# Attention's gated sum put off, experts' weights split by whole chunks, one-hots begun earlier

## The chip, the cores and the metric

One NeuronCore of a Trainium2 chip runs the whole program. The metric is the device time of one execution in microseconds; of the profiled execution the span is told too, from the first to the last instruction. TensorE is PE, VectorE DVE, ScalarE ACT, GpSimd POOL; SP is the queue that issues most of the DMAs.

## What is computed

One layer over 1024 latent tokens of width 1024 with 256 context tokens: a normalized, modulated input goes through one projection into latent attention (8 heads, 128 + 64 wide keys) and a bidirectional mLSTM; both are gated, summed and projected, and a residual is added. Then a mixture of 16 SwiGLU experts follows in which each expert takes its best 128 tokens, and a last norm.

```python
y_mla = attend(q, concat([k_ctx, k_lat]), concat([v_ctx, v_lat]))        # softmax over 1280 keys
out   = (sigmoid(g_mla) * y_mla + sigmoid(g_ml) * y_ml) @ w_out
x     = x + g1 * out
aff   = softmax(h @ w_router);  g, idx = top_k(aff.T, 128)               # each expert picks its tokens
a, u  = xs @ w_e_gate, xs @ w_e_up                                       # xs = h[idx], 128 x 1024
y     = (silu(a) * u) @ w_e_down * g                                     # added back at idx
```

All matrix products of weights are done in three passes of a 32-bit format (fp32r): a value is split into a high part (ACT's cast) and a low part (DVE's subtraction of the cast from the value), and high x high, high x low and low x high are summed in PSUM.

## The kernel before

Each engine has one queue in order. The order in it is laid down when the program is built, by a planner that takes ready instructions by priority (program order, raised inside `high_priority`) against costs of its own; `issue_after(x)` makes what follows stand behind x on x's engine.

**Attention** (line 1425 on) goes in 32 steps g: head g // 4, 256 queries each. A step's `scores` makes five PSUM tiles of 128 keys x 2 and a running maximum over them on DVE: one reduction (1529), four `tensor_max` (1532), a halving (1536). `peak` turns the maximum on PE (1545) and reduces it (1548); `peak2` writes the row into the queries' extra rows (1560, 1561); `exps` adds it through PE, exponentiates on ACT, casts the high parts, and lets POOL sum the five exponentials (1590, 1592). Meanwhile the step before is finished: `low` makes low parts of its exponentials on DVE (1599), `values` and `values2` are PE's products, `weigh` and `weigh2` make the weight of a query out of the sum (1623 to 1630), and `finish` multiplies (1635) and adds the gated result to the accumulator in SBUF (1636).

**Experts.** `Weights` (line 770 on) streams 16 x 12 chunks of 1 MB (128 partitions x 2 x 1024): eight of gate and up (two halves of the hidden width, four chunks each), four of down. Raw chunks go round `N_RAW` = 16 buffers and two single ones (`ONCE`); `split` casts and subtracts half a chunk at a time (128 x 1024, lines 875 and 876) into a ring of `N_HI` = 4 pairs of high and low. `products` (1305) asks for the split of the half four ahead, for loads further on, and issues 12 matmuls of 512 columns a chunk (through the helper line 1190). `pick(e)` builds eight one-hot tiles 128 x 128 of the tokens of expert e on POOL (1257; on DVE for e = 0), multiplies them on PE with a table to get row numbers and gates (1263), makes these into integers on DVE (1270 to 1275) and gathers the rows by an indirect DMA of POOL (1278). `turn_x` and `turn` are PE transposes with a cast and a subtraction (1287 to 1290). `y` (1353) scales an expert's result, and POOL's indirect DMA adds it to DRAM (1354).

In the loop over experts the order is: four gate/up chunks, `act` (silu on ACT 1315, product on DVE 1316), four more with the transposes of the first hidden half inside, and `pick(e + 2)` after the second of these (the sixth chunk); then four down chunks D0 to D3 with the transposes of the second half after D0, and those of the next expert's tokens after D1 and D2; then `y` and the scatter.

Before the experts, `Merge.rest` prepares three half chunks with the subtraction on POOL (`W.split(N_HI - 1, G)`) while DVE sorts the routing weights; a fourth is split by DVE behind `counted`, and the slots of the tokens follow behind that.

Of the kernel before, what the change touches and what calls it, by code (L numbers as in the profile page):

```python
# [33 lines left out]
P = 128  # L34
# [24 lines left out]

N_HAP, N_EARLY, N_MID, N_LATE, N_HI = 2, 3, 4, 7, 4  # L60
N_RAW = N_HAP + N_EARLY + N_MID + N_LATE
# [708 lines left out]
class Weights:  # L770
# [34 lines left out]
    def load(self, upto):  # L805
        while self.loaded < min(upto, 12 * NE):
            j = self.loaded
            j = SEQ[j] if j < len(SEQ) else j
            src = self.source(j)
            if j in ONCE:  # L810
                t = self.once[j]
                loads = [self.nc.sync.dma_start(t[c], src[:, c, :]) for c in range(self.begun.pop(j, 0), 2)]
            else:
                b = self.buffer(SEQ.index(j) if j < len(SEQ) else j - 2)
                t = b[:, 0], b[:, 1]
                if len(b.shape) == 4:
                    src = src.rearrange("p a (c d) -> p a c d", d=256)
                loads = [self.nc.sync.dma_start(b, src)]
            if self.after is not None:
                for x in loads:  # L820
                    self.tc.add_manual_dep(x.ins, self.after.ins.name,
                                           mybir.DependencyInfo(mybir.DependencyClass.Sync, mybir.DependencyReason.DATA),
                                           reason="what is awaited goes before")
                if j >= N_RAW + 2 or j in (ONCE[0], 14, 15, 16, 17):
                    self.after = None
            self.raw[j] = t
            self.loaded += 1
# [30 lines left out]
    def halves(self):  # L858
        return [self.hi.tile([P, D], F32R, name=x, bufs=N_HI) for x in ("hi", "lo")]

    def split(self, upto, engine=None):

        while self.cut < min(upto, 24 * NE):
            j, c = divmod(self.cut, 2)
            self.load((SEQ.index(j) if j < len(SEQ) else j) + 1)
            w = self.raw[j][c]
            if self.cut < 24 * NE - 8:
                hi, lo = self.halves()
            else:
                both = self.buffer(self.cut - 12 * NE + 6, F32R)  # L870
                hi, lo = both[:, 0, :], both[:, 1, :]
            self.parts[self.cut] = hi, lo
            if len(w.shape) == 3:
                hi, lo = [t.rearrange("p (c d) -> p c d", d=256) for t in (hi, lo)]
            self.nc.scalar.copy(hi, w)  # L875
            done = (engine or self.nc.vector).tensor_sub(lo, w, hi)  # L876
            self.cut += 1
            if self.cut == upto:
                return done
# [90 lines left out]
class Merge:  # L970
# [81 lines left out]
    def rest(self, aff, thr, pool):  # L1052
# [109 lines left out]
        for i in range(8):  # L1162
            project(i)
            if i > 0:
                store_h(i - 1)
            if i < 7:
                self.source(i + 1)
            W.load((1, 3, 6, 6, 7, 7, 9, 9)[i])
        W.load(N_RAW - 1)
        self.sb.close()  # L1170
        W.hi = pool("p7a")
        t = W.wide_hi(F32)
        W.once[ONCE[0]] = t[:, 0, :], t[:, 1, :]
        W.split(N_HI - 1, G)
        with tc.high_priority():
# [9 lines left out]
def moe(tc, A, out, aff, thr, W, h2_d, acc_d, ident, rstd, dump):  # L1185
# [6 lines left out]
    with ExitStack() as st:  # L1192
# [43 lines left out]
        with tc.issue_after(counted.ins):  # L1236
            done = W.split(N_HI)

# [11 lines left out]
        V.scalar_tensor_tensor(slot, taken[:, :, 0, :], -1.0, taken[:, :, 1, :], op0=ALU.add, op1=ALU.add)  # L1250
        gat, idx, xg, xsT, hid = {}, {}, {}, {}, {}

        def pick(e):
            oh = W.narrow().bitcast(BF16).rearrange("p (a b) -> p a b", b=P)
            for o in range(8):
                if e > 0:
                    G.tensor_scalar(oh[:, o, :], iota, slot[:, o, e:e + 1], None, op0=ALU.is_equal)  # L1257
            for o in range(0, 8, 4) if e == 0 else ():
                V.tensor_tensor(oh[:, o:o + 4], iota[:, None, :].to_broadcast([P, 4, P]),
                                slot[:, o:o + 4, e:e + 1].to_broadcast([P, 4, P]), op=ALU.is_equal)  # L1260
            ap = ps7.tile([P, 512], F32, name="tr", bufs=2)
            for i in range(8):
                done = mm(ap[:, :5], oh[:, i, :], aux[:, i, e, :], i == 0, i == 7)
            if e == 0:
                with tc.issue_after(done.ins):
                    ps = ps7.tile([P, 512], F32, name="pu", bufs=2)
                    for x in range(11):
                        mm(ps, W.parts[0][0][:, :P], W.parts[0][0][:, :512], True, True)
            ax = p7.tile([P, 8], F32, name="ax", bufs=3)
            V.tensor_copy(ax[:, :5], ap[:, :5])  # L1270
            idx[e] = p7.tile([P, 1], I32, name="idx", bufs=4)
            gat[e] = p7.tile([P, 1], F32, name="gt", bufs=4)
            V.scalar_tensor_tensor(idx[e], ax[:, 0:1], 128.0, ax[:, 1:2], op0=ALU.mult, op1=ALU.add)
            V.tensor_add(gat[e], ax[:, 2:3], ax[:, 3:4])
            picked = V.tensor_add(gat[e], gat[e], ax[:, 4:5])
            dump("idx", idx[e], lambda o: o[:, e:e + 1])
            xg[e] = p7.tile([P, D], F32, name="xg", bufs=2)
            got = G.indirect_dma_start(out=xg[e], out_offset=None, in_=h2_d,
                                 in_offset=bass.IndirectOffsetOnAxis(ap=idx[e][:, :1], axis=0))
            with tc.issue_after(got.ins):  # L1280
                return picked, got, G.memset(ax[:, 7:8], 0.0)
# [15 lines left out]
        def products(j, ps, l, start, stop):  # L1297

            for c in range(2):
                W.split(2 * j + c + N_HI)  # L1300
                if c == 0:
                    W.load(N_RAW + j + 4 - sum(o < j + 2 for o in ONCE))
                wh, wl = W.parts.pop(2 * j + c)
                k = 2 * (j % 4) + c
                lh, ll = l[0][:, k, :], l[1][:, k, :]
                for o in range(2):
                    r = slice(o * 512, o * 512 + 512)
                    mm(ps[o], lh, wh[:, r], start and c == 0, False)
                    mm(ps[o], lh, wl[:, r], False, False)
                for o in range(2):  # L1310
                    mm(ps[o], ll, wh[:, slice(o * 512, o * 512 + 512)], False, stop and c == 1)

        def act(pa, pu):
# [3 lines left out]
            return h  # L1317

        picked, got, W.after = pick(0)
        for q in range(2):  # L1320
            turn_x(0, q)
        urgent.__exit__(None, None, None)
        with tc.issue_after(W.after.ins):
            pick(1)
        for e in range(NE):
# [3 lines left out]
            for hf in range(2):  # L1329
                ps = [ps7.tile([P, 512], F32, name=x, bufs=2) for x in ("pa", "pu")]  # L1330
                for q in range(4):
                    products(j + 4 * hf + q, ps, xsT[e], q == 0, q == 3)
                    if hf == 1 and q == (2 if e == 0 else 0):
                        t = W.wide_hi(F32R)
                        hd += [t[:, x, :].rearrange("p (a b) -> p a b", b=P) for x in range(2)]
                        turn(hs[0], *hd, 0)
                    if hf == 1 and q == 1 and e + 2 < NE:
                        pick(e + 2)
                hs.append(act(*ps))
            py = [ps7.tile([P, 512], F32, name=f"py{o}", bufs=1) for o in range(2)]  # L1340
            if e + 1 < NE:
                for q in range(4):
# [3 lines left out]
                    if q == 0:  # L1346
                        turn(hs[1], *hd, 1)
                    if q in (1, 2):
                        turn_x(e + 1, q - 1)
# [16 lines left out]
            for m in range(4):  # L1366
                x = W.middle(m)
                for a in range(2):
                    i = 2 * m + a
                    nc.sync.dma_start(x[:, a], acc_d[i * P:(i + 1) * P].rearrange("p (c d) -> p c d", d=256))  # L1370
                xs += [x[:, 0], x[:, 1]]
# [12 lines left out]
            def write(i):  # L1384
                scale(i, xs[i])
                stores.append(nc.sync.dma_start(out[i * P:(i + 1) * P].rearrange("p (c d) -> p c d", d=256), xs[i]))

            W.split(24 * NE)
            z = p7.tile([P, D], F32, name="xg", bufs=2)
            for o in range(2):  # L1390
                c = slice(o * 512, o * 512 + 512)
                for k in range(8):
                    wh, wl = [w[:, c] for w in W.parts[2 * j + 16 + k]]
                    mm(py[o], hd[0][:, k, :], wh, k == 0, False)
# [30 lines left out]
def attention(tc, A, xc, qn_d, qp_d, kv, kpe, g1_d, ident, ones, ml, weights, follow):  # L1425
# [12 lines left out]
    with tc.tile_pool(name="p5", bufs=1, reuse_waits="tile") as p5, \  # L1438
# [5 lines left out]
        NG = 4 * HEADS  # L1444
        vh, vl, K, Q, G1, PS, MX, TH, SUM, W, PV = {}, {}, {}, {}, {}, {}, {}, {}, {}, {}, {}

# [111 lines left out]
        def peak2(g):  # L1558
# [3 lines left out]
            with tc.issue_after(cut.ins):  # L1562
                for p in PARTS[2:]:
                    low(g - 1, p)

        def exps(g):
# [60 lines left out]
        def weigh2(g):  # L1627
            tr = along(*W[g])
            w = W[g] = p5.tile([P, 256], F32, name="w", bufs=2)
            V.tensor_mul(w, tr, G1[g // 2][:, cols(g)])  # L1630

        def finish(g):
            h, c = g // 4, slice((g % 4) * 256, (g % 4) * 256 + 256)
            w = W.pop(g)
            V.tensor_mul(w, PV.pop(g), w)
            V.tensor_add(xc[h][:, c], xc[h][:, c], w)

# [406 lines left out]
```

## Time and profile before

| | us |
|---|---|
| median of 3 runs (2039.46 to 2044.31) | 2041.03 |
| the profiled execution | 2041.3 |
| its span | 2039.5 |
| PE busy, share of the span | 1910.6, 94% |
| DVE busy | 1462.2, 72% |
| ACT busy | 1048.9, 51% |
| POOL busy | 602.0, 30% |
| mean granted clock of PE | 0.979 |

Shares are averages over stages with different limits; what a change in one stage is worth is read from that stage's own rows. In a timeline a row is: start, length, engine, line, operation, output and inputs, shapes, how many instructions were merged into the row, and in brackets how long the engine stood idle before it and what ended that.

### The profile page before, as it was taken

The numbers are of one execution on the slowest core, as the hardware profiler recorded it, in microseconds if no ns is written. First come the engines' busy times: TensorE is split into PE (matmuls) and PEld (weight loads), VectorE is DVE, ScalarE is ACT, GpSimd is POOL, SyncE is SP. The second block draws the span as 40 slices with busy tenths as digits, with TensorE's granted clock in tenths as the row PEclk, the third lists the DMA queues.
The fourth block names the chain that finished last, engine by engine and source line by source line (L and its number), as shares of the span: only waits on it lengthen the run. The fifth ranks groups of instructions, "written<-read, shape, count | busy, mean of one in ns | idle before, by whom it ended". The sixth has DMA issues, their size and how long they took to land. (4 is left out here: it accounts for less than half of the span.)

```text
span 2039.5 us, 28755 instructions
## 1 busy us (share of the span) xinstructions
PE 1910.6 (94%) x10458; PEld 1614.1 (79%) x10458; DVE 1462.2 (72%) x2704; ACT 1048.9 (51%) x1677; POOL 602.0 (30%) x527
## 2 busy tenths in 40 slices
PE   7999999999999999899999998985999999999994
PEld 3898888888877878889998987863778778787873
DVE  6454555112477888687877788578899999999997
ACT  5554421123247676434334434321777777777774
POOL 0000000000043040275434446433453634536310
PEclk9999999999999999999999998997999999999997
DMA  7143376222187060323111111636899999999975
GB/s 302 58 149 100 106 248 220 76 93 89 61 279 248 22 221 1 94 71 117 50 47 50 37 53 58 246 133 224 292 375 380 372 381 369 383 382 364 388 240 187
DMA packets 156301, 385.84 MB, mean 189 GB/s; under 512 B 10224, under 2 KB 94784, under 8 KB 137088
## 3 DMA queue, kind: packets, MB, share of 16 engines
q1 hardware_dynamic: 141104, 329.73, 44.9%
q0 software_dynamic: 12752, 45.90, 7.4%
q10 hardware_dynamic: 2304, 8.39, 1.1%
q8 instruction: 82, 1.34, 0.3%
q14 instruction: 59, 0.48, 0.1%
HBM read 327.04 MB, written 56.93 MB: 188 GB/s over the span
## 5 line engine op out<-in xcount | busy, mean ns | idle before, releaser
L86 PE MATMUL mm<-hT,whi 128*128 128x512 f32 (+1 forms) x1392 | 414.8, 381 | 2.6 <-DVE hT L305 2.3
L86 PEld LDWEIGHTS mm<-hT,whi 128*128 128x128 f32 x1392 | 255.1, 189 | 52.0 <-DVE hT L305 2.4
L86 PE MATMUL mm<-hT,wlo 128*128 128x512 f32 (+1 forms) x696 | 262.9, 378 | 0.3 <-DVE wlo L90 0.3
L876 DVE TENSOR_TENSOR lo<-raw_l,hi 128x1024 fp32r<-128x1024 f32 x156 | 188.1, 1235 | 11.2 <-ACT hi L875 8.2
L1257 POOL TENSOR_SCALAR g<-iota,slot 128x128 bf16<-128x128 f32 x120 | 192.4, 1624 | 0.0
L875 ACT CAST hi<-raw_l 128x1024 fp32r<-128x1024 f32 x156 | 163.3, 1053 | 48.2 <-PE pu L1190 33.8
L1190 PE MATMUL py<-hi,hd 128*128 128x512 f32 x480 | 160.8, 399 | 0.0
L86 PEld LDWEIGHTS mm<-hT,wlo 128*128 128x128 f32 x696 | 131.2, 189 | 24.5 <-DVE wlo L90 0.7
L90 DVE TENSOR_TENSOR wlo<-wraw,whi 128x1024 fp32r<-128x1024 f32 x38 | 46.5, 1224 | 142.8 <-ACT whi L89 142.8
L1590 POOL TENSOR_TENSOR es<-es,e 128x512 f32<-128x512 f32 x96 | 126.4, 1317 | 7.0
L1590 POOL TENSOR_TENSOR es<-e 128x512 f32<-128x512 f32 x32 | 41.8, 1305 | 272.4 <-ACT e L1584 272.4
L876 DVE TENSOR_TENSOR lo<-xca,hi 128x1024 fp32r<-128x1024 f32 x96 | 115.3, 1231 | 6.6 <-ACT hi L875 4.8
L1584 ACT ACTIVATE e<-s 128x512 f32<-128x512 f32 x160 | 94.5, 612 | 47.1 <-PE s L1432 47.1
L1354 POOL DMA_INDIRECT acc_d<-y,idx x15 | 34.9, 2328 | 270.4 <-DVE y L1353 270.4
L875 ACT CAST hi<-xca 128x1024 fp32r<-128x1024 f32 x96 | 100.1, 1051 | 27.6 <-PE pu L1190 20.0
L89 ACT CAST whi<-wraw 128x1024 fp32r<-128x1024 f32 x38 | 40.0, 1051 | 128.8 <-PE mm L86 120.4
L1190 PEld LDWEIGHTS py<-hi,hd 128*128 128x128 f32 x480 | 89.7, 188 | 17.9
L1190 PE MATMUL pa<-hi,xh 128*128 128x512 f32 x256 | 102.4, 400 | 0.3 <-ACT xh L1289 0.3
L1190 PE MATMUL pa<-lo,xh 128*128 128x512 f32 x256 | 99.9, 390 | 1.1 <-DVE lo L876 1.1
L1190 PE MATMUL pu<-lo,xh 128*128 128x512 f32 x256 | 99.8, 390 | 0.0
L1190 PE MATMUL pu<-hi,xl 128*128 128x512 f32 x256 | 99.8, 390 | 0.0
L1190 PE MATMUL pa<-hi,xl 128*128 128x512 f32 x256 | 99.7, 390 | 0.0
(509 smaller groups left out, 5088.2 us busy)
## 6 DMA issues: line engine op xcount, KB each, us to landing
raw_l<-in_wgu SPq DMA_DIRECT2D x54, 1024.0 KB
xca<-in_wgu SPq DMA_DIRECT2D x33, 1024.0 KB
raw_l<-in_wd SPq DMA_DIRECT2D x28, 1024.0 KB
raw_e<-in_wgu SPq DMA_DIRECT2D x24, 1024.0 KB
wraw<-in_win SPq DMA_DIRECT2D x38, 512.0 KB
wt<-in_wmod_b SPq DMA_DIRECT2D x32, 512.0 KB
ha<-in_wgu SPq DMA_DIRECT2D x16, 1024.0 KB
xca<-in_wd SPq DMA_DIRECT2D x15, 1024.0 KB
```

The costliest lines, as they stand in the source:

```text
L86: return TE.matmul(o, l, r, start=start, stop=stop, skip_group_check=True)
L89: S.copy(hi, raw)
L90: V.tensor_sub(lo, raw, hi)
L875: self.nc.scalar.copy(hi, w)
L876: done = (engine or self.nc.vector).tensor_sub(lo, w, hi)
L1190: return TE.matmul(o, l, r, start=start, stop=stop, skip_group_check=True)
L1257: G.tensor_scalar(oh[:, o, :], iota, slot[:, o, e:e + 1], None, op0=ALU.is_equal)
L1354: G.indirect_dma_start(out=acc_d, out_offset=bass.IndirectOffsetOnAxis(ap=idx[e][:, :1], axis=0), in_=y, in_offset=None, compute_op=ALU.add)
L1584: S.activation(E[p], ps, AF.Exp)
L1590: G.tensor_add(s, E[0] if p == 1 else s, E[p])
```

## The change

Three parts.

1. The addition of `finish` (line 1636) is no longer made at the end of its pass through the loop but in the `peak2` of the next pass, behind the low part that is made there; the last two steps add at once. The ring of the product has three buffers instead of two.
2. `split` casts and subtracts a whole chunk (128 x 2048) at a time; the ring holds three whole chunks (`N_HI` = 3) instead of four halves. The memory comes from the raw buffers: `N_EARLY` goes from 3 to 1, so `N_RAW` from 16 to 14. Before the experts, one whole chunk is prepared on POOL and a second on DVE, instead of three halves and one. The last expert's last chunks and the rows for the last norm move to other buffers.
3. `pick` is cut in two. `mark(e + 2)` builds the one-hots and is called after the fourth chunk of an expert; `pick(e + 2)`, the products with the table and the gather, is called after D1, the tenth.

```diff
-N_HAP, N_EARLY, N_MID, N_LATE, N_HI = 2, 3, 4, 7, 4
+N_HAP, N_EARLY, N_MID, N_LATE, N_HI = 2, 1, 4, 7, 3
...
     def halves(self):
-        return [self.hi.tile([P, D], F32R, name=x, bufs=N_HI) for x in ("hi", "lo")]
+        return [self.hi.tile([P, 2, D], F32R, name=x, bufs=N_HI) for x in ("hi", "lo")]
...
     def split(self, upto, engine=None):
-        while self.cut < min(upto, 24 * NE):
-            j, c = divmod(self.cut, 2)
+        while self.cut < min(upto, 12 * NE):
+            j = self.cut
             self.load((SEQ.index(j) if j < len(SEQ) else j) + 1)
-            w = self.raw[j][c]
-            if self.cut < 24 * NE - 8:
+            raw = self.raw[j]
+            if not 12 * NE - 4 <= j < 12 * NE - 2:
                 hi, lo = self.halves()
             else:
-                both = self.buffer(self.cut - 12 * NE + 6, F32R)
-                hi, lo = both[:, 0, :], both[:, 1, :]
-            self.parts[self.cut] = hi, lo
...
-            self.nc.scalar.copy(hi, w)
-            done = (engine or self.nc.vector).tensor_sub(lo, w, hi)
+                hi, lo = [self.buffer(2 * j - 12 * NE + 6 + x, F32R) for x in range(2)]
+            self.parts[j] = hi, lo
...
+            for h, l, w in views:
+                self.nc.scalar.copy(h, w)
+                done = (engine or self.nc.vector).tensor_sub(l, w, h)
...
-            W.load((1, 3, 6, 6, 7, 7, 9, 9)[i])
+            W.load((1, 3, 4, 4, 5, 5, 7, 7)[i])
...
-        W.split(N_HI - 1, G)
+        W.split(1, G)
...
         with tc.issue_after(counted.ins):
-            done = W.split(N_HI)
+            done = W.split(2)
...
-        def pick(e):
-            oh = W.narrow().bitcast(BF16).rearrange("p (a b) -> p a b", b=P)
+        def mark(e):
+            oh = marks[e] = W.narrow().bitcast(BF16).rearrange("p (a b) -> p a b", b=P)
             for o in range(8):
                 if e > 0:
                     G.tensor_scalar(oh[:, o, :], iota, slot[:, o, e:e + 1], None, op0=ALU.is_equal)
...
+        def pick(e):
+            oh = marks.pop(e)
             ap = ps7.tile([P, 512], F32, name="tr", bufs=2)
...
         def products(j, ps, l, start, stop):
 
+            W.split(j + N_HI)
+            W.load(N_RAW + j + N_HI + 2 - sum(o < j + N_HI for o in ONCE))
+            both = W.parts.pop(j)
             for c in range(2):
-                W.split(2 * j + c + N_HI)
-                if c == 0:
-                    W.load(N_RAW + j + 4 - sum(o < j + 2 for o in ONCE))
-                wh, wl = W.parts.pop(2 * j + c)
+                wh, wl = both[0][:, c], both[1][:, c]
...
+        mark(0)
         picked, got, W.after = pick(0)
...
         with tc.issue_after(W.after.ins):
+            mark(1)
             pick(1)
...
-                    if hf == 1 and q == 1 and e + 2 < NE:
-                        pick(e + 2)
+                    if hf == 0 and q == 3 and e + 2 < NE:
+                        mark(e + 2)
...
+                    if q == 1 and e + 2 < NE:
+                        pick(e + 2)
                     if q in (1, 2):
                         turn_x(e + 1, q - 1)
...
             with tc.issue_after(cut.ins):
                 for p in PARTS[2:]:
                     low(g - 1, p)
+                if g > 1:
+                    add(g - 2)
...
-            w = W[g] = p5.tile([P, 256], F32, name="w", bufs=2)
+            w = W[g] = p5.tile([P, 256], F32, name="w", bufs=3)
...
             V.tensor_mul(w, PV.pop(g), w)
-            V.tensor_add(xc[h][:, c], xc[h][:, c], w)
+            ADD[g] = xc[h][:, c], w
+            if g >= NG - 2:
+                add(g)
+
+        def add(g):
+            if g in ADD:
+                x, w = ADD.pop(g)
+                V.tensor_add(x, x, w)
```

## Rows read from the trace of the kernel before

**Rows 1.** Table of stretches: busy us (instructions) of each engine, clock, DMA share, GB/s.

```profile
core 0: us, PE busy (x) PEld busy (x) DVE busy (x) ACT busy (x) POOL busy (x), PEclk, DMA share, GB/s
...
826.00:1262.00 436.00, 412.74 (x3090) 385.54 (x3088) 336.50 (x572) 177.75 (x350) 216.70 (x186) 1.00 0.18 58
...
1434.00:1996.00 562.00, 546.63 (x2607) 447.91 (x2608) 523.39 (x555) 434.99 (x467) 237.09 (x158) 1.00 0.98 358
```

**Rows 2.** Table of waits, 860 to 1240: total us, times, longest.

```profile
PE sm L1545 <- DVE mm L1536: 14.3, 26, 1.0
```

**Rows 3.** Table of waits, 1440 to 1996.

```profile
PE tr L1190 <- POOL g L1257: 13.6, 12, 1.1
```

**Rows 4.** Timeline of DVE, one step of attention.

```profile
1099.15 1.40 DVE L1636 TENSOR_TENSOR xca<-xca,w 128x256 f32<-128x256 f32 x1
1100.47 3.05 DVE L1532 TENSOR_TENSOR mx<-mx,s 128x512 f32<-128x512 f32 x4
1103.56 0.61 DVE L1536 TENSOR_TENSOR mm<-mx 128x256 f32<-128x256 f32 x1
1104.10 0.68 DVE L1599 TENSOR_TENSOR tl<-e,th 128x512 fp32r<-128x512 f32 x1
1104.70 0.42 DVE L1548 TENSOR_REDUCE mq<-sm 128x2 f32<-128x256 f32 x1
```

**Rows 5.** Timeline of POOL, the same step.

```profile
1101.78 1.30 POOL L1590 TENSOR_TENSOR es<-es,e 128x512 f32<-128x512 f32 x1
1103.15 0.74 POOL L1592 TENSOR_TENSOR eh<-es 128x256 f32<-128x256 f32 x1
```

**Rows 6.** Timeline of PE, the same step.

```profile
1102.00 0.28 PE L1432 MATMUL s<-qp,kpe 128*128 128x256 f32 x1
...
1103.42 0.28 PE L1432 MATMUL pv<-th,vl 128*128 128x256 f32 x1
1104.23 0.44 PE L1545 MATMUL sm<-ident,mm 128*128 128x128 f32 x2 [0.52 <-DVE mm L1536]
...
1105.37 0.38 PE L1555 MATMUL sm<-ident,mq 128*128 128x128 f32 x2
```

**Rows 7.** Timeline of POOL before the experts.

```profile
1401.50 4.64 POOL L876 TENSOR_TENSOR lo<-ha,hi 128x1024 fp32r<-128x1024 f32 x2 [11.54 <-ACT hi L875]
1408.54 2.38 POOL L876 TENSOR_TENSOR lo<-ha,hi 128x1024 fp32r<-128x1024 f32 x1 [2.40 <-ACT hi L875]
```

**Rows 8.** Timeline of DVE before the experts.

```profile
1423.49 1.21 DVE L876 TENSOR_TENSOR lo<-ha,hi 128x1024 fp32r<-128x1024 f32 x1
```

**Rows 9.** Timeline of PE, the row sums of two experts in turn.

```profile
1886.14 0.54 PE L1190 MATMUL tr<-aux,g 128*128 128x5 bf16 x7
1887.82 0.18 PE L1190 MATMUL tr<-aux,g 128*128 128x5 bf16 x1 [1.13 <-POOL g L1257]
...
1922.50 0.35 PE L1190 MATMUL tr<-aux,g 128*128 128x5 bf16 x8
```

**Rows 10.** The chain that ended last: D0, the next expert's first chunk, its D0.

```profile
1893.56 2.72 PE py L1190 x12
...
1905.87 0.45 PE pa L1190 x2
...
1928.45 2.72 PE py L1190 x12
```

**Rows 11.** Timeline of POOL, the one-hots of one expert.

```profile
1873.90 13.86 POOL L1257 TENSOR_SCALAR g<-iota,slot 128x128 bf16<-128x128 f32 x8
```

**Rows 12.** Timeline of ACT, two casts behind the last transposes of down.

```profile
1903.64 2.00 ACT L875 CAST hi<-raw_l 128x1024 fp32r<-128x1024 f32 x2
```

**Rows 13.** Timeline of DVE, an expert's y and a pair of subtractions.

```profile
1870.42 1.40 DVE L1353 SCALAR_TENSOR_TENSOR y<-py,gt,g2row 128x512 f32<-128x512 f32 x2
...
1901.52 2.36 DVE L876 TENSOR_TENSOR lo<-raw_l,hi 128x1024 fp32r<-128x1024 f32 x2 [0.24 <-ACT hi L875]
```

**Rows 14.** Timeline of PE, first chunks of the expert after the last pick.

```profile
1944.49 0.50 PE L1190 MATMUL pa<-lo,xh 128*128 128x512 f32 x1 [0.52 <-DVE lo L876]
```

More of the change, by code (lines that the diff above doesn't have):

```diff
@@ L809, in load @@
             src = self.source(j)
-            if j in ONCE:
+            if j == ONCE[0]:
+                t = self.once[j]
+                loads = [self.nc.sync.dma_start(t, src)]
+            elif j == ONCE[1]:
                 t = self.once[j]
@@ L813, in load @@
             else:
-                b = self.buffer(SEQ.index(j) if j < len(SEQ) else j - 2)
-                t = b[:, 0], b[:, 1]
+                t = b = self.buffer(SEQ.index(j) if j < len(SEQ) else j - 2)
                 if len(b.shape) == 4:
@@ L823, in load @@
                                            reason="what is awaited goes before")
-                if j >= N_RAW + 2 or j in (ONCE[0], 14, 15, 16, 17):
+                if j >= N_RAW + 2 or j in (ONCE[0], *range(N_RAW - 2, N_RAW + 2)):
                     self.after = None
@@ L858, in halves @@
     def halves(self):
-        return [self.hi.tile([P, D], F32R, name=x, bufs=N_HI) for x in ("hi", "lo")]
+        return [self.hi.tile([P, 2, D], F32R, name=x, bufs=N_HI) for x in ("hi", "lo")]
     def split(self, upto, engine=None):
-        while self.cut < min(upto, 24 * NE):
-            j, c = divmod(self.cut, 2)
+        while self.cut < min(upto, 12 * NE):
+            j = self.cut
             self.load((SEQ.index(j) if j < len(SEQ) else j) + 1)
-            w = self.raw[j][c]
-            if self.cut < 24 * NE - 8:
+            raw = self.raw[j]
+            if not 12 * NE - 4 <= j < 12 * NE - 2:
                 hi, lo = self.halves()
             else:
-                both = self.buffer(self.cut - 12 * NE + 6, F32R)
-                hi, lo = both[:, 0, :], both[:, 1, :]
-            self.parts[self.cut] = hi, lo
-            if len(w.shape) == 3:
-                hi, lo = [t.rearrange("p (c d) -> p c d", d=256) for t in (hi, lo)]
-            self.nc.scalar.copy(hi, w)
-            done = (engine or self.nc.vector).tensor_sub(lo, w, hi)
+                hi, lo = [self.buffer(2 * j - 12 * NE + 6 + x, F32R) for x in range(2)]
+            self.parts[j] = hi, lo
+            if j == ONCE[1]:
+                views = [(hi[:, c], lo[:, c], raw[c]) for c in range(2)]
+            elif len(raw.shape) == 4:
+                views = [[t.rearrange("p a (c d) -> p a c d", d=256) for t in (hi, lo)] + [raw]]
+            else:
+                views = [(hi, lo, raw)]
+            for h, l, w in views:
+                self.nc.scalar.copy(h, w)
+                done = (engine or self.nc.vector).tensor_sub(l, w, h)
             self.cut += 1
@@ L1172, in rest @@
         t = W.wide_hi(F32)
-        W.once[ONCE[0]] = t[:, 0, :], t[:, 1, :]
-        W.split(N_HI - 1, G)
+        W.once[ONCE[0]] = t
+        W.split(1, G)
         with tc.high_priority():
@@ L1250, in moe @@
         V.scalar_tensor_tensor(slot, taken[:, :, 0, :], -1.0, taken[:, :, 1, :], op0=ALU.add, op1=ALU.add)
-        gat, idx, xg, xsT, hid = {}, {}, {}, {}, {}
-        def pick(e):
-            oh = W.narrow().bitcast(BF16).rearrange("p (a b) -> p a b", b=P)
+        gat, idx, xg, xsT, marks = {}, {}, {}, {}, {}
+        def mark(e):
+            oh = marks[e] = W.narrow().bitcast(BF16).rearrange("p (a b) -> p a b", b=P)
             for o in range(8):
@@ L1267, in pick @@
                     for x in range(11):
-                        mm(ps, W.parts[0][0][:, :P], W.parts[0][0][:, :512], True, True)
+                        mm(ps, W.parts[0][0][:, 0, :P], W.parts[0][0][:, 0, :512], True, True)
             ax = p7.tile([P, 8], F32, name="ax", bufs=3)
@@ L1366, in moe @@
             for m in range(4):
-                x = W.middle(m)
+                x = W.buffer(12 * NE + 2 + m)
                 for a in range(2):
                     i = 2 * m + a
-                    nc.sync.dma_start(x[:, a], acc_d[i * P:(i + 1) * P].rearrange("p (c d) -> p c d", d=256))
+                    nc.sync.dma_start(x[:, a], acc_d[i * P:(i + 1) * P])
                 xs += [x[:, 0], x[:, 1]]
@@ L1385, in write @@
                 scale(i, xs[i])
-                stores.append(nc.sync.dma_start(out[i * P:(i + 1) * P].rearrange("p (c d) -> p c d", d=256), xs[i]))
-            W.split(24 * NE)
+                stores.append(nc.sync.dma_start(out[i * P:(i + 1) * P], xs[i]))
+            W.split(12 * NE)
             z = p7.tile([P, D], F32, name="xg", bufs=2)
@@ L1392, in moe @@
                 for k in range(8):
-                    wh, wl = [w[:, c] for w in W.parts[2 * j + 16 + k]]
+                    wh, wl = [w[:, k % 2, c] for w in W.parts[j + 8 + k // 2]]
                     mm(py[o], hd[0][:, k, :], wh, k == 0, False)
@@ L1444, in attention @@
         NG = 4 * HEADS
-        vh, vl, K, Q, G1, PS, MX, TH, SUM, W, PV = {}, {}, {}, {}, {}, {}, {}, {}, {}, {}, {}
+        vh, vl, K, Q, G1, PS, MX, TH, SUM, W, PV, ADD = {}, {}, {}, {}, {}, {}, {}, {}, {}, {}, {}, {}
         def big():
```

## The prediction

> **What bounds the kernel now.** I read the table of stretches first [rows 1]: TensorE (PE) is busy 412.7 of 436 us in attention (826 to 1262) and 546.6 of 562 us in the experts (1434 to 1996), so what can be won there is PE's holes. DVE is busy 523 of the same 562 us: whatever frees PE meets DVE next. The table of waits then names the holes. In attention the transposes of line 1545 wait for DVE's last maximum, 26 times between 860 and 1240 [rows 2]. In the experts the row sums of line 1263 wait for POOL's one-hots, 12 times [rows 3]; no row of that table has a cast waiting for a load.
>
> **Part 1, the gated sum.** One step of attention, DVE's timeline [rows 4]: the sum of line 1636 stands between the first maximum and the other four. It takes 1.40 us for 256 elements, where the final halving of the maxima, of the same size, takes 0.61 and a 512-element subtraction 0.68. POOL shows why [rows 5]: the halving starts at 1103.56 and ends at 1104.17, 0.28 after POOL's op 1103.15 + 0.74 = 1103.89. DVE ops with both inputs in SBUF finish 0.28 after the POOL op they meet; those that read PSUM run at 0.69 to 0.79 apiece.
> PE [rows 6] starts its last values matmul at 1103.42 and the transposes at 1104.23: 0.81, where neighbouring matmuls stand 0.12 apart. Hole: 0.69. 26 x 0.69 = 17.9 us is all there is.
> Without the sum, the first maximum is out of the way by 1099.15 and the four follow PE. The last scores matmul starts at 1102.00 and takes 0.28, so the last maximum starts at about 1102.31, not 1102.84 (1100.47 + 3.05 - 0.69), and the halving 0.72 later (1103.56 less 1102.84), at 1103.03. POOL's op in front ended at 1101.78 + 1.30 = 1103.08 (0.06 earlier if the sum no longer cuts in), and the next starts 0.07 later. So the halving meets either the end of the one (done by 1103.4, PE's hole gone) or the start of the other (done at 1104.1, nothing won). It is a close race; the step pitch differs from step to step, and I expect the former in some 21 of 26.
> Where the stall goes: then the 512-element subtraction meets POOL's last op, ends some 0.28 + 0.27 after it (about 1104.4), and the next maximum (1104.70 now, 0.42 long) starts behind it, at about 1104.3. PE wants it at 1105.37 - 0.69 = 1104.68; it is there at 1104.75 to 1105.0. Loss 0.1 to 0.35. Per step I take 0.69 less 0.2, in 21 of 26, the rest nothing: 10.3 us. The holes are not alike: the longest idle in the table is 1.0 us [rows 2] against 0.52 in this step, and for the longer ones I add 2.7. **13 us**; bounds 2 (race lost everywhere) and 20.
> The sum itself goes behind the third subtraction, after POOL's five ops of the step: 0.42 instead of 1.40. It pushes the reduction of line 1623 by some 0.35. PE needs that reduction only after ten more matmuls of 0.12: hidden; without that cover it would cost 0.35 x 26 = 9 us. The third buffer for the product costs no time.
> The Trainium skill (SBUF — State Buffer, Who interferes with whom) says of a DVE instruction with two SBUF inputs against a POOL instruction that reads SBUF that the order of issue decides and the loser waits for the whole other instruction; the 0.28 behind 1103.89 agrees.
>
> **Part 2, before the experts.** POOL's three half-chunk subtractions [rows 7] (4.64 for two, 2.38 for one) become one whole chunk, about 4.6 us, an estimate from the two. DVE's small ops of the routing are held by each. The last block, 2.38 less 0.2, goes: -2.2 us. Against it, the split that DVE does before the slots becomes a whole chunk: 1.21 [rows 8] becomes 2.27 (a 512-element subtraction 0.68, 1024 1.21, so 1.06 more): +1.06. Sum **-1.1 us**; bounds 0 and -2.2.
>
> **Part 3, the one-hots.** PE's row sums [rows 9]: seven at 1886.14, the eighth after 1.13 idle at 1887.82; one expert on, all eight at 1922.50 within 0.35. The pitch of these two is 36.36 us; the pitch of the chain over the next expert, which had no such wait, is 1928.45 - 1893.56 = 34.89 [rows 10]. The wait costs 1.47 us an expert, 12 times: 17.6 us. POOL needs 13.86 us for its eight, from 1873.90 on [rows 11], behind the scatter of the expert before, and that start does not move: it hangs on y. What moves is the use, from the sixth chunk to the tenth: second down chunk, D0 + 2.72 + 0.44 + 2.72 = 1899.4. 25.5 us (24 when the pitch is shorter) are there for 13.86. The wait goes.
>
> **Part 4, whole chunks.** 384 casts and 384 subtractions become 192 each. A pair of casts takes 2.00 back to back [rows 12], a whole one about the same; a pair of subtractions 2.36 [rows 13], a whole one 2.27: DVE gains 0.1 a chunk, 1 us an expert, off the path. The path is latency. Three chunks in the ring: the cast of a chunk starts when the third one before it is through PE; 2.00 + 2.27 and 0.3 for the hand-overs (my allowance) are 4.6 us; PE wants the low part two chunks plus one matmul later, 5.44 + 0.23 = 5.67. Slack 1.1 us (halves: 1.05 + 1.21 + 0.3 = 2.55 against three halves, 4.08, and 0.23: 1.75). In the gate and up chunks that holds. At the down chunks more stands in the queues. Count from D0 = 0, pick in D1 (0.21): next expert's chunks G0 at 12.5 (1905.87 - 1893.56 + 0.21), G1 15.2, G2 18.0. ACT casts for G1 from 10.3 (1903.64 - 1893.56 + 0.21) to 12.3; DVE subtracts to 14.7, does y (1.40 [rows 13]) to 16.0, subtracts for G2 to 18.25; needed at 18.2. Wait 0.05 to 0.1. If DVE's planned order puts y first: y to 13.95, G1's low part at 16.2, needed at 15.45: 0.75. The trace has this once the one-hots no longer hold PE: 1944.49, idle 0.52 behind DVE [rows 14]. I take 0.35 an expert; bounds 0.05 and 0.75.
> Sum of parts 3 and 4: 12 x (1.47 - 0.35) = 13.4; two experts had neither wait (-0.7), the last two lose 0.35 of their 0.7 (+0.7): **13.4 us**; bounds 9 and 18.
> Loads: the same megabytes; chunk buffers fall from 18 to 16, and each load still waits for DVE. DMA is 0.98 busy at 358 GB/s over the stage [rows 1]; 3% more pace, if it could not be had, would eat 0.03 x 190 = 6 chunks of the stock over the whole stage, which 16 buffers cover. Without that cover the 13 us would be lost. The last expert's buffers and the final loads move to other slots, free long before: nothing.
>
> **Sum.** 13 + 1.1 + 13.4 = 27.5. The profiled execution took 2041.3 (span 2039.5 and 1.8 around it), the median is 2041.0: 2013.5 by the median.
>
> **Rivals.**
> B: the race of part 1 is lost: the halving meets POOL's last op (0.74 + 0.28). For it: the margin is 0.05 us. Against: the pitch varies. Attention gives 2: 2041 - 2 - 14.5 = 2024.
> C: DVE takes the place of the one-hots: y and the longer subtractions make PE wait 1.1 or more an expert. For it: DVE 523 of 562, slack down from 1.75 to 1.1, and the row at 1944.49. Against: it gains 1 us an expert. 12 x (1.47 - 1.1) = 4.4 won, 2 lost in the other experts: 2041 - 13 - 1 - 4.4 + 2 = 2025.
> D, slower: longer DVE subtractions starve POOL's one-hots. In the rows one of the eight takes 13.86 / 8 = 1.73, up to 2.4, two half subtractions (most of them run back to back). If it stays "two subtractions", a one-hot takes 4.6, eight 37 us, with scatter and gather 40 an expert: 13 x 4 more, 2041 - 14 + 52 = 2079. It decides from 24 / 8 = 3.0 us on (PE waits again), and from about 4.2 us, where an expert takes 1.1 us more than now, the kernel is slower. Against: PE paces DVE at 2.72 with 2.27 of work, so there is a gap in each chunk. The rule of the Trainium skill (SBUF — State Buffer, Who interferes with whom) would have a one-hot wait for one whole subtraction, 2.27 and its own work, which is just in time; no run here shows it yet.
> E: B and C together, or the waits return elsewhere: 2036 to 2041.
>
> **Chances.** As forecast 0.62 (its own range 2004 to 2020), B 0.15, C 0.13, D 0.04, E 0.06. The range to hold 8 in 10 reaches down to 2004 (bounds 20 + 2 + 15) and up to 2027, past B and C. 0.2%, 4 us, is about what a measurement of this kernel tells from no change: faster 0.92, same 0.03 (half of E), slower 0.05.
>
> **What would show it.** Right: line 1545 without waits on line 1536 in most steps, the sum at 0.42 in its new place, no wait on the one-hots, a pitch of the down chunks of 34.9 to 35.3 us. Wrong: halvings still 0.6 long; a PE wait on the low parts in the first chunks of an expert; one-hots of 3 us and more; casts that wait for a load.

## The result and the profile after

The changed kernel takes 2024.86 us (median of 4 runs, 2022.23 to 2026.43) against 2041.2: ratio 0.9917, 95% interval 0.99 to 0.9934, so 16 us faster where 27.5 were forecast. Its profiled execution has a span of 2024.3 against 2039.5. Cut at the same instructions of both traces, the 15.2 us split as follows (us; the halving is DVE's last maximum of a step, the count is `counted`, the reduction that opens the making of the slots):

| stretch | before | after | change | forecast |
|---|---|---|---|---|
| start to the halving of attention's step 1 | 847.15 | 847.37 | +0.2 | 0 |
| to the halving of step 30 | 386.09 | 379.16 | -6.9 | -13 |
| to the count | 189.98 | 189.65 | -0.3 | -2.2 |
| to the first expert's y | 47.15 | 51.43 | +4.3 | +1.1 |
| to the fifteenth expert's y | 506.97 | 495.78 | -11.2 | -13.4 |
| to the end | 62.18 | 60.93 | -1.3 | 0 |

The first and the third stretch vary by up to 3.2 and 4.6 us between kernels that do not touch them (847.2 to 850.4; 185.0 to 189.7 in those that prepare whole chunks), the others by 0.7 at most. So single stretches of a trace are compared here, and whole spans only to some 5 us.

Table of stretches after, the columns of [rows 1]: PE's holes of 23 us in attention and 15 in the experts have shrunk to 19 and 7.

```profile
826.00:1262.00 436.00, 417.35 (x3095) 386.88 (x3094) 326.05 (x578) 178.89 (x350) 225.81 (x188) 0.99 0.19 60
1434.00:1996.00 562.00, 555.30 (x2642) 452.18 (x2641) 511.02 (x370) 410.38 (x289) 284.34 (x151) 1.00 0.99 362
```

Table of waits after, 860 to 1240, beside [rows 2]; PEld is the weight load ahead of a matmul, so its idle time overlaps PE's work:

```profile
PEld sm L1567 <- DVE mq L1560: 14.6, 27, 0.6
...
PE sm L1567 <- DVE mq L1560: 3.7, 22, 0.2
PE sm L1557 <- DVE mm L1548: 2.3, 2, 1.2
```

The wait for the halving, 14.3 us, is 2.3. In its place the next transposes wait for the reduction of the peaks (line 1548 before, 1560 now); the same table of before has for it:

```profile
PEld sm L1555 <- DVE mq L1548: 2.5, 6, 0.7
```

One step shows why. Timelines of DVE, POOL and PE, after, beside [rows 4 to 6]:

```profile
1098.80 0.69 DVE L1544 TENSOR_TENSOR mx<-mx,s 128x512 f32<-128x512 f32 x1 [0.25 <-PE s L1444]
1099.52 0.42 DVE L1548 TENSOR_TENSOR mm<-mx 128x256 f32<-128x256 f32 x1
1099.86 1.22 DVE L1613 TENSOR_TENSOR tl<-e,th 128x512 fp32r<-128x512 f32 x1
1101.00 0.41 DVE L1560 TENSOR_REDUCE mq<-sm 128x2 f32<-128x256 f32 x1
```
```profile
1099.57 0.96 POOL L1606 TENSOR_TENSOR eh<-es 128x256 f32<-128x256 f32 x1
```
```profile
1100.02 0.41 PE L1557 MATMUL sm<-ident,mm 128*128 128x128 f32 x2
1100.27 1.03 PE L1444 MATMUL pv<-e,vf 128*128 128x256 f32 x4
1101.47 0.43 PE L1567 MATMUL sm<-ident,mq 128*128 128x128 f32 x2 [0.17 <-DVE mq L1560]
```

The halving has won the race (0.42, and the transposes follow at once). The subtraction behind it meets POOL's last sum, ends 0.55 after that sum's end (1101.08 against 1100.53) and holds the reduction up.

The moved sum has a price of its own, in the steps that also make keys for the next head. DVE and PE after, in such a step:

```profile
1091.20 0.42 DVE L1657 TENSOR_TENSOR xca<-xca,w 128x256 f32<-128x256 f32 x1
1091.65 0.42 DVE L1448 TENSOR_TENSOR kl<-s,kh 128x256 fp32r<-128x256 f32 x1
```
```profile
1092.22 0.41 PE L1635 MATMUL s<-ident,eh 128*128 128x128 f32 x2 [0.23 <-DVE kl L1448]
```

The sum (line 1657 now) stands ahead of the keys' low part `kl`, and the transposes of `weigh` wait for that. PE is idle so for 1.8 us in 8 steps (waits of PE, 845 to 1262), for 0.2 us in one step before.

Table of waits after, 1440 to 1996, beside [rows 3]:

```profile
PEld tr L1295 <- DVE hd L1298: 12.3, 13, 1.0
...
PE tr L1295 <- DVE hd L1298: 6.6, 13, 0.5
```

The wait for the one-hots is gone. They take longer than in [rows 11], 15.4 us (POOL's timeline), and have time for it:

```profile
1472.17 15.39 POOL L1262 TENSOR_SCALAR g<-iota,slot 128x128 bf16<-128x128 f32 x8
```

A new wait stands in each of 13 experts, at the transposes of the next expert's tokens. Timelines of DVE and PE after, in the second down chunk of the first expert:

```profile
1457.36 2.29 DVE L881 TENSOR_TENSOR lo<-raw_l,hi 128x2048 fp32r<-128x2048 f32 x1 [0.17 <-ACT hi L880]
1459.57 0.68 DVE L1298 TENSOR_TENSOR hd<-tr,hd 128x512 fp32r<-128x512 f32 x1
```
```profile
1458.40 0.35 PE L1195 MATMUL tr<-aux,g 128*128 128x5 bf16 x8
...
1459.39 0.39 PE L1195 MATMUL py<-lo,hd 128*128 128x512 f32 x1
1460.31 0.65 PE L1295 MATMUL tr<-ident,xg 128*128 128x128 f32 x4 [0.53 <-DVE hd L1298]
```

The PSUM ring `tr` has two buffers, given out in turn. One holds the transposes of the hidden units, whose low part stands on DVE behind a whole-chunk subtraction; the row sums, moved to this place, take the other; the third tenant waits. From the last matmul's start to the transposes' start are 0.92 us where matmuls stand 0.23 apart: some 0.7 an expert.

DVE's timeline before the first expert, beside [rows 8]:

```profile
1416.46 2.28 DVE L881 TENSOR_TENSOR lo<-ha,hi 128x2048 fp32r<-128x2048 f32 x1
1418.66 0.41 DVE L1253 SCALAR_TENSOR_TENSOR g<-tr,mk 128x256 f32<-128x256 f32 x1
1418.99 2.28 DVE L881 TENSOR_TENSOR lo<-raw_e,hi 128x2048 fp32r<-128x2048 f32 x1
1421.19 0.28 DVE L1255 SCALAR_TENSOR_TENSOR slot<-g 128x128 f32<-128x128 f32 x1
```

Two whole-chunk subtractions stand on the way to the slots: the one that the change enlarged, and the third chunk's, which the planner put between the two instructions that make the slots.

### The profile page after: what moved, and what is told of

The parts are those of the page before. It is cut to its first block, busy times and chain, and to the rows that moved or that the text cites. A ratio compares the mean times of both kernels' runs of the same rounds, so it can differ in the third digit from the quotient of the medians.

```text
span 2024.3 us, 28212 instructions
## 1 busy us (share of the span) xinstructions
PE 1912.3 (94%) x10458; PEld 1610.8 (80%) x10458; DVE 1424.3 (70%) x2515; ACT 1016.2 (50%) x1486; POOL 653.1 (32%) x525
## 5 line engine op out<-in xcount | busy, mean ns | idle before, releaser
L881 DVE TENSOR_TENSOR lo<-raw_l,hi 128x2048 fp32r<-128x2048 f32 x92 | 210.3, 2292 | 23.7 <-ACT hi L880 22.5
L1262 POOL TENSOR_SCALAR g<-iota,slot 128x128 bf16<-128x128 f32 x120 | 210.6, 1770 | 0.0
L880 ACT CAST hi<-raw_l 128x2048 fp32r<-128x2048 f32 x92 | 176.1, 1914 | 55.0 <-PE pu L1195 33.0
L1195 PE MATMUL py<-hi,hd 128*128 128x512 f32 x496 | 168.3, 401 | 0.0
L881 DVE TENSOR_TENSOR lo<-xca,hi 128x2048 fp32r<-128x2048 f32 x54 | 123.5, 2292 | 16.4 <-ACT hi L880 15.5
L880 ACT CAST hi<-xca 128x2048 fp32r<-128x2048 f32 x54 | 102.9, 1908 | 35.3 <-PE pu L1195 21.6
L1544 DVE TENSOR_TENSOR mx<-mx,s 128x512 f32<-128x512 f32 x128 | 87.9, 686 | 27.2 <-PE s L1444 24.6
```

The lines of the kernel that those rows point to most:

```text
L880: self.nc.scalar.copy(h, w)
L881: done = (engine or self.nc.vector).tensor_sub(l, w, h)
L1195: return TE.matmul(o, l, r, start=start, stop=stop, skip_group_check=True)
L1544: V.tensor_max(new if p > 1 else new.rearrange("p (a b) -> p a b", a=2), old, ps if p > 1 else ps.rearrange("p (a b) -> p a b", a=2))
```

## The experiments

**One part at a time.** The first kernel is before with the diff's `add(g)` alone; the second is after with the sum back in `finish`.

> The kernel before with the gated sum put off and nothing else. Theory: the last step of attention begins its value matmuls 6.8 us earlier in the trace of after, and all of that comes from the gated sum, so 2041.2 - 6.8 = 2034.4 (2033 to 2036). Rival, the two parts work on each other, because the gain had grown to 7.8 us by the merge: 2033 or less. The prediction's own term was 13 us: 2028.

> The kernel after with the gated sum back in its old place, so that only the experts' parts of the change are left. Theory: it has the rest of the 16.3 us, 9.5, so 2041.2 - 9.5 = 2031.7 (2030 to 2033). The prediction's terms for the experts were 1.1 + 13.4 us: 2026.7. Rival, the earlier start of the weights' loads in after is worth something to the experts: above 2033.

Measured: 2035.46 (ratio 0.9975, 0.9966 to 0.9984) and 2033.17 (0.9959, 0.9945 to 0.9972). Each kernel has the stretches of after where it has after's edit, and those of before elsewhere: halving to halving 379.38 with the sum moved and 385.40 with the experts' parts alone; count to first y 47.26 and 51.40; first to fifteenth y 507.02 and 495.81. So in the stretches that they touch the parts do not work on each other. By the whole times they win 4.1 and 6.4 us, 10.5 of the 16.3; in both traces the stretch from the start to the second halving, which neither edit touches, is 849.5 to 850.0 us, 2.2 to 2.8 longer than in before and after.

**The two halves of the experts' part.** After with one-hots and row sums in their old place, and before with them in the new place and half chunks:

```diff
-                    if hf == 0 and q == 3 and e + 2 < NE:
+                    if hf == 1 and q == 1 and e + 2 < NE:
                         mark(e + 2)
+                        pick(e + 2)
```

> The kernel after with the one-hots and the row sums back in their old place, so that of the experts' part only the whole chunks are left. Theory (GpSimd gets in once at each boundary of two VectorE instructions, so a one-hot takes 2.4 us behind whole subtractions instead of 1.7): eight take 19 us instead of 13.9, TensorE's wait grows from 1.5 to 6 or 7 us in each of 12 experts, and the kernel is slower than before by 30 to 60 us less the 5 us that attention gives: 2065 to 2095. Rival (VectorE leaves a gap in each chunk, and the whole chunks cost the one-hots nothing): 2034 to 2038.

> The kernel before with the one-hots begun earlier and the row sums in the second down chunk, and nothing else: half chunks, and the gated sum in its old place. Theory (the later row sums alone take the 1.47 us wait away, and half subtractions hold the hidden units' low part up by less): pitch 35.1 to 35.3 instead of 36.38, 12 x 1.15 = 14 us: 2026 (2024 to 2029). Rival (the whole chunks are needed for it, since half ones leave the low parts too little slack in the first chunks): pitch 35.6 to 36.4, 2031 to 2041.

Measured: 2065.26 (1.012, 1.0103 to 1.0137) and 2021.31 (0.9906, 0.989 to 0.9923). The pitch of the experts, the time from one y to the next, can be read from DVE's y, one line of each trace's view by line between 1560 and 1660; from the first to the last start are two pitches (one in the second row) and 0.66, in the order after, whole chunks with the old place, half chunks with the new:

```profile
L1365 DVE SCALAR_TENSOR_TENSOR y<-py,gt,g2row x6: 739/741/741, 1574.4 to 1646.2; 128x512 f32<-128x512 f32 x6
```
```profile
L1364 DVE SCALAR_TENSOR_TENSOR y<-py,gt,g2row x4: 740/742/744, 1584.1 to 1624.6; 128x512 f32<-128x512 f32 x4
```
```profile
L1360 DVE SCALAR_TENSOR_TENSOR y<-py,gt,g2row x6: 740/744/746, 1573.2 to 1643.5; 128x512 f32<-128x512 f32 x6
```

| pitch, us | row sums in the sixth chunk | in the tenth |
|---|---|---|
| half chunks | 36.37 (before) | 34.80 |
| whole chunks | 38.2 to 39.9 | 35.59 (after) |

The earlier one-hots and later row sums are worth 19.0 us from the first to the fifteenth y (506.97 to 487.95) and leave PE without a wait in these experts, which is more than that kernel's theory gave (pitch 35.1 to 35.3). The whole chunks lose 7.8 of that (495.78), and 4.4 before the first y (47.06 against 51.43). The theory for the whole chunks alone had the direction, not the cause. POOL, before and in that kernel:

```profile
1581.20 2.33 POOL L1354 DMA_INDIRECT acc_d<-y,idx  x1 [17.18 <-DVE y L1353]
1583.01 13.85 POOL L1257 TENSOR_SCALAR g<-iota,slot 128x128 bf16<-128x128 f32 x8
```
```profile
1585.73 3.39 POOL L1365 DMA_INDIRECT acc_d<-y,idx  x1 [18.08 <-DVE y L1364]
1588.61 13.35 POOL L1262 TENSOR_SCALAR g<-iota,slot 128x128 bf16<-128x128 f32 x8
```

The eight one-hots take 13.35 us there, not 19. They start 2.9 us behind the start of the scatter instead of 1.8, since the scatter takes 3.39 us instead of 2.33. The row sums keep PE idle for 2.3 us in each of eleven experts (1.1 before), not 6; the rest of the longer pitch are waits for low parts, of the hidden units above all (4.3 us of idle PE, 12 times).

**What the new wait is made of.** First the row sums go to another ring, then the hidden units' low part also goes ahead of the next subtraction, then, on after itself, only the subtractions are halved:

```diff
-            ap = ps7.tile([P, 512], F32, name="tr", bufs=2)
+            ap = ps7.tile([P, 512], F32, name="pu" if e > 1 else "tr", bufs=2)
...
-                        turn(hs[1], *hd, 1)
+                        with tc.issue_after(turn(hs[1], *hd, 1).ins):
+                            W.split(j + 9 + N_HI)
...
-                done = (engine or self.nc.vector).tensor_sub(l, w, h)
+                for c in range(2) if j != ONCE[1] else (slice(None),):
+                    done = (engine or self.nc.vector).tensor_sub(l[:, c], w[:, c], h[:, c])
```

> The kernel after, but the index matmuls of experts 2 to 15 write into a buffer of pu's ring instead of tr's. Theory (two buffers for three tenants): the transposes of the next expert's tokens no longer wait for VectorE's low part of the hidden units, 0.68 us in each of 13 experts, 8.8 us: 2016 (2014 to 2018). Rival (VectorE is late as such, the wait only moves): the matmuls that read the late low parts wait instead, less than 2 us gained: 2023 to 2025.

> The kernel with pick's results in pu's ring, and besides the low part of the second half of the hidden units ahead of the whole-chunk subtraction on VectorE. Theory (what is left of the wait is the 2.29 us subtraction ahead of that low part): the pitch of the experts falls from 35.20 to 34.9 us, so 13 x 0.3 = 4 us less than 2021.1: 2017 (2015.5 to 2019). Rival (VectorE is so full that its idle microsecond ahead of the low part comes back as a wait for a later chunk's low part): pitch 35.2 or more, 2020 to 2024.

> The kernel after with each whole chunk's subtraction in two halves on VectorE (whole casts and whole buffers stay). Theory (the length of one VectorE instruction ahead of the hidden units' low part is what the whole chunks cost): the low part comes 1 us earlier, pitch 34.8 to 35.0 instead of 35.59, some 8 us: 2017 (2015 to 2019). Rival (the whole casts and buffers, handed over once a chunk, are what makes VectorE late): pitch above 35.3.

Measured: 2021.07 (0.9906, 0.9891 to 0.9921), pitch 35.20; 2016.78 (0.9876, 0.986 to 0.9893), pitch 34.80; 2021.66 (0.9912, 0.9896 to 0.9929), pitch 34.86. With the other ring the wait at the transposes is gone, and half of it stands at the matmuls that read the late low part (waits, 1440 to 1850):

```profile
PEld py L1195 <- DVE hd L1298: 6.2, 11, 0.6
```

So theory and rival shared it: of 0.79 us an expert, 0.39 were the ring and 0.40 the low part behind the long instruction. With the low part first both are gone. Halved subtractions do the same without a change of ring, up to the ninth pitch; the last three are 36.9 to 37.2 us, with PE waiting for low parts, and the stretch to the fifteenth y (495.2) is no shorter than in after. ACT's timeline shows where these late low parts come from, in the fifth expert and in the fourteenth:

```profile
1576.72 0.60 ACT L1324 ACTIVATE g<-pa 128x512 f32<-128x512 f32 x1 [0.53 <-PE pa L1196]
```
```profile
1894.31 0.60 ACT L1324 ACTIVATE g<-pa 128x512 f32<-128x512 f32 x1 [3.45 <-PE pa L1196]
1894.81 1.89 ACT L880 CAST hi<-xca 128x2048 fp32r<-128x2048 f32 x1
```

From the second half of the twelfth expert on the planner put the silu one cast earlier into ACT's queue. ACT stands idle at it until PE is through, 1.9 us the first time and 2.8 to 3.5 from then on, and the cast behind it, with its low part, is late by that. No run tests this order by itself.

**Before the first expert.** The third chunk's subtraction goes behind the one-hots of expert 0, and in a second kernel behind `picked`, the last of the gate sums:

```diff
+            with tc.issue_after(first.ins) if j == 0 else ExitStack():
-            W.split(j + N_HI)
+                W.split(j + N_HI)
```

> The kernel after, but the third chunk's subtraction (2.29 us) stands behind the first expert's one-hots on VectorE instead of between the two steps that make the slots. Theory (it lies on the path to the first expert): the first y comes 2.3 us earlier, and the whole is about 2.3 us shorter: 2022.6. Rival (the first expert waits for a later low part instead): the first y comes less than 1 us earlier.

> The kernel after with the third chunk's subtraction behind the first expert's index and gate sums on VectorE, so that the load which waits for its buffer is issued behind the first gather. Theory (in the run with the subtraction behind the one-hots, that load's 1 MB was issued 0.5 us ahead of the gather and held its rows up by 4.5 us): gather to transposes 4.5 us again, and from the count to the first y 49 us instead of 51.4. Rival (the gather is slow whenever a load runs beside it): gather to transposes 7 us or more, 53 us or more to the first y.

Measured: 2031.34 (0.9948, 0.9931 to 0.9966) and 2026.37 (0.9935, 0.9918 to 0.9951); count to first y 57.46 and 53.67 against 51.43. Both lose, though the slots come 2.1 us earlier in both. In the first, the subtraction now holds up the index sums (gather 4.43 behind the slots, 2.67 in after), and more is lost behind it, as the timelines of SP, POOL and PE show:

```profile
1423.43 0.33 SPq L820 DMA_DIRECT2D raw_e<-in_wgu  x1
```
```profile
1423.95 1.08 POOL L1287 DMA_INDIRECT xg<-h_d,idx  x1 [7.83 <-DVE gt L1284]
```
```profile
1421.39 4.10 PE L1195 MATMUL pu<-hi 128*128 128x512 f32 x11
1433.05 1.94 PE L1296 MATMUL tr<-ident,xg 128*128 128x128 f32 x8 [7.56 <-DMA xg<-h_d,idx]
```

The subtraction frees the buffer of a 1 MB load, which is issued 0.5 us ahead of the gather: the transposes start 8.0 us after the gather's issue ends, 3.5 in after, where that load is issued 2.6 us ahead of the gather. The second kernel puts the load behind the gather, POOL, PE and the stretch from 1428:

```profile
1419.54 3.14 POOL L1286 DMA_INDIRECT xg<-h_d,idx  x1 [6.07 <-DVE gt L1283]
```
```profile
1418.72 4.12 PE L1195 MATMUL pu<-hi 128*128 128x512 f32 x11
1426.21 1.94 PE L1295 MATMUL tr<-ident,xg 128*128 128x128 f32 x8 [3.37 <-DMA xg<-h_d,idx]
```
```profile
1428.00:1432.00 4.00, 4.00 (x18) 2.94 (x18) 2.46 (x6) 0.59 (x1) 4.00 (x8) 0.51 1.01 428
```

From the issue's end to the transposes are 3.5 us again, so the load just ahead of the gather was the cause of the 8.0. But the gather's issue takes 3.14 instead of 1.08 beside the subtraction that now runs with it (1419.44 to 1421.73 on DVE), so that from the issue's start to the transposes it is 6.7 us, near the rival's 7 and not the theory's 4.5. And PE, idle for 3.4 us after its eleven fill-in matmuls, goes on at the lower granted clock (0.51; 1.00 in after from 1428 on). Against the 2.1 won stand 2.1 at the gather and 2.2 from the transposes to y.

**The reduction of the peaks.** After with the first low part behind it:

```diff
-            with tc.issue_after(halved.ins):
-                low(g - 1, 0)
...
             with tc.issue_after(found.ins):
+                low(g - 1, 0)
                 low(g - 1, PARTS[1])
```

> The kernel after, but in attention the first low part's subtraction stands behind the reduction of the peaks instead of ahead of it. Theory (the reduction is late because the subtraction ahead of it meets GpSimd's last sum): TensorE's wait for the peaks falls by 0.43 us in each of some 26 steps, 11 us: 2014 (2011 to 2018). Rival 1 (the collision only moves: the reduction or the next matmuls wait for the same subtraction later): 2022 to 2026. Rival 2 (the low parts come too late for their matmuls): slower than 2026.

Measured: 2019.44 (0.9903, 0.9888 to 0.9918); halving to halving 374.66 against 379.16. A step of it, DVE and POOL:

```profile
1097.60 0.42 DVE L1548 TENSOR_TENSOR mm<-mx 128x256 f32<-128x256 f32 x1
1098.55 0.42 DVE L1558 TENSOR_REDUCE mq<-sm 128x2 f32<-128x256 f32 x1 [0.53 <-PE sm L1555]
1098.89 1.28 DVE L1612 TENSOR_TENSOR tl<-e,th 128x512 fp32r<-128x512 f32 x2
```
```profile
1097.65 0.96 POOL L1605 TENSOR_TENSOR eh<-es 128x256 f32<-128x256 f32 x1
```

DVE waits for PE now, and two subtractions take 1.28 behind POOL's sum. Count as a hole what a matmul of PE starts later than is usual (the median) behind the kind of matmul ahead of it. Over 29 steps the holes ahead of these transposes fall from 8.7 us to 0.1, but those ahead of the products with low parts grow from 6.8 to 9.4 and those at `weigh`'s transposes from 4.6 to 6.2: 4.5 us are won, not 11.

**All that won, put together:** before with the gated sum moved, the low part behind the reduction, one-hots early, half chunks kept.

> The kernel before with the gated sum put off, the first low part behind the reduction of the peaks, and the one-hots begun early; the half chunks stay. Theory (the parts add, and the whole chunks were a loss): 6.8 us from the gated sum, 4.6 from the low part's place, 19.0 from the one-hots, so 2040 - 30.4 = 2009.6 (2007 to 2013); pitch of the experts 34.8. Rival (the gains overlap, since VectorE and the loads get less time in each stage): 2014 or more.

Measured: 2009.8 (2008.92 to 2010.71), ratio 0.9852, 0.9835 to 0.9868; 374.47 halving to halving, 47.25 to the first y, 487.94 to the fifteenth. It beats both kernels, and in these stretches the parts add up.

## Why the prediction was right and where it was not

The sign and the wide range (2004 to 2027) held, and so did the mechanisms of the moved sum and of the earlier one-hots. The size was too large by 11 us, in three terms, and 2024.86 lies outside the forecast's own range of 2004 to 2020. That it stands beside the numbers of rivals B (2024) and C (2025) is luck: the losses have other causes.

1. Part 1, 13 us, measured 6.9: the mechanism was right, and the race was won in as many steps as forecast (of 26 holes of over 0.08 us ahead of the halving's transposes 5 are left). The term "0.69 less 0.2, in 21 of 26" with its 2.7 on top was mis-sized. Holes in PE, 29 steps, counted as above: ahead of the halving's transposes they fell from 19.5 to 4.5 us, 15.0 won where 17.2 gross were forecast. Ahead of the transposes of the reduction they grew from 1.8 to 8.7, 6.9 lost where 4.2 were forecast; the run with the low part moved shows that cause. And 1.9 us are lost at `weigh`'s transposes, behind the keys' low part, where the prediction had the moved sum as "hidden": the wait is there with the sum moved alone and not with the experts' parts alone.
2. Part 2, 1.1 us won, measured 4.3 lost ahead of the first y: the step that failed is "becomes a whole chunk: +1.06" as the whole cost. That term was right (1.0), but the third chunk's subtraction moved in behind it, 2.1 us more, and the first expert takes 1.5 longer from its first low part to its y. Of that, 0.8 are waits of PE, the one at the transposes above all (from its first matmul to the next expert's first 36.10 us, 35.31 before); the rest is y itself, which starts later on DVE. The block that POOL saves did not come back as 2.2 us; the stretch that holds it is 0.3 shorter, within its scatter. The kernel with half chunks has 47.06 here.
3. Parts 3 and 4, 13.4 us, measured 11.2, from two terms that were both off: the one-hots' wait was worth 19.0 (17.6 forecast), the whole chunks cost 0.79 an expert, past the bound of 0.75, where 0.35 was taken. The step that failed is where part 4 put that cost: at the next expert's first low parts, behind y. It stood at the transposes after D1, where part 3's own move had added a third tenant to a ring of two, and where the longer subtraction delays the hidden units' low part. Each edit was costed by itself. The wait for the ring needs both: it is in neither of the kernels with one of them. The late low part comes with the whole chunks alone too, as the kernel with the row sums in their old place shows.

Rival D did not come: a one-hot takes 2.40 us (median of eight) beside whole subtractions of 2.29, 1.67 before. The rule of the Trainium skill (SBUF — State Buffer, Who interferes with whom), by which the loser waits for one whole instruction, agrees with that. Rival C named the right engine, and with 0.8 an expert the outcome lies between it and the forecast; B did not come, since the holes at the halving are gone. No cast waited for a load, as forecast; in two faster kernels with whole casts and the 16 buffers, the ones with a pitch of 34.8 to 34.9, three and four casts did, for 0.8 to 1.0 us.

## What to carry to other kernels

When an edit moves an allocation, count the tenants of its ring between the new place and the next request, and look at what stands on the releasing engine's queue at that moment; a longer instruction there delays every release behind it. Halving an instruction count is no gain on an engine that is off the path, and a cost where short, urgent work is queued behind it. An instruction that frees a buffer also issues a load: before moving it, see what that load will stand in front of.

## What was not expected of the hardware

- PE began on the rows of a gather that was issued 0.5 us behind a 1 MB load 8.0 us after the end of its issue; with that load 2.6 us ahead of it, or behind it, 3.5.
- An indirect DMA's issue on POOL took 3.14 us beside a subtraction of two SBUF inputs on DVE and 1.08 without; the scatter of an expert took 2.33 beside half subtractions and 3.39 beside whole ones (in the kernel with halved subtractions 2.33 in twelve of fifteen, 8.0 in the other three).
- After 3.4 us without work PE went on at the lower of its two clocks, 1.2 GHz: its first matmuls started 0.42 apart, 0.23 in after.
